# One step of a hybrid decoder: more expert blocks beside the gates, a layer's modulation computed elsewhere, slot transposes with a set place

## The chip, the cores and the metric

The kernel runs on one core of a Trainium2 chip. The metric is the device time of one execution in microseconds (us). The engines are TensorE (PE in the rows; PEld is its weight load), VectorE (DVE), ScalarE (ACT), GpSimd (POOL) and SyncE (SP). Each works through its own list of instructions in a fixed order, which a scheduler lays down when the kernel is built; an instruction that has to wait holds up those behind it on its engine.

## What is computed

Two layers of a decoder work on 576 tokens: a prompt of 512 and eight sampled sequences of 8. Cut to what matters here:

```
for l in range(2):
    mod = c @ w_ada + b_ada                      # modulation: shift, scale, gate, six parts
    hn  = rmsnorm(x) * (1 + scale1) + shift1
    proj = hn @ w_in                             # six parts: recurrence, short convolution, gates
    merged = sigmoid(ga) * rglru(conv(xa)) + sigmoid(gb) * (bg * conv(cg * xs))
    x  = x + g1 * (merged @ w_out)
    h  = rmsnorm(x) * (1 + scale2) + shift2
    # experts: per head the 16 best of 128 x 128 product keys
    idx, gate = top16(scores(h @ w_q, sub_keys))
    x  = x + g2 * sum_k gate_k * gelu(u_tab[idx_k] . h) * v_tab[idx_k]
y = rmsnorm(x)
```

There are 16384 experts a layer, in 128 blocks of 128. All products are exact to float32: an operand is split into a high and a low part and three products are added.

## The kernel before

**Tokens.** Of the 512 prompt tokens the first 384 (`TD`) go the dense way: all experts are computed for them and weighted with a gate matrix that is zero where an expert wasn't chosen. The last 128 and the 64 samples go by gathers: for each token and choice a row of `u_tab` and one of `v_tab` is fetched by GpSimd (`rows_of`, L659; 128 rows, 512 KB at a time) and used on VectorE (`udot` L665, `vsum` L676). These gathers are tasks in a list (`gtasks`). `pump` (L157) adds a number to a credit and hands out one task for each whole credit; calls of it stand all over the kernel, with rates from L65: `MPUMP` in the mixer, `QRATE` in the queries, `ARATE` in slots and gates, `BPUMP` per block in the second phase. What is left at the end of a layer is handed out in one go (L1039). A task's VectorE part is held behind the last split that was traced before it (`anchor`).

**A layer** runs through these stages, whose times are the profile's:

1. `mixer`. For 8 column groups six projections each (`proj`, L388). With each projection `beside` (L369) draws steps of a generator that runs the samples through the same layer (`chain`, `SIDE` steps a projection, 56 in all); when the chain is spent, it pumps gathers. In layer 0 it also computes one chunk of modulation: `ada` (L170) loads 1 MB of weights, multiplies, and evicts to a tile in the tag `rows`, which has five buffers that the gathered rows use too; `bring` (L196) turns the result to where it belongs. A layer has 24 chunks; 36 are done here, 16 of layer 0 and 20 of layer 1.
2. `queries` (L822): the second norm, the last four chunks of layer 1's modulation (layer 0 only), queries, scores and best 16.
3. `dense_slots` (L895): VectorE combines the halves (`combine`, L750), TensorE transposes the result into slots (L907), for three sets of 128 tokens.
4. `phase_a` (L911): the first `NA` expert blocks are multiplied with the tokens (`u_mm`, L707) and sent through a GELU. The first `NS_` of them go to DRAM (`ad`), the last 16 stay in SBUF, in two buffers of the tag `at`. Beside it the gate matrix is made in 24 pieces (`gate_piece`, L920): VectorE makes one-hot tiles (L930) and products (L935), TensorE multiplies them (L940), and the pieces go to DRAM. The odd ones of the first 18 use the `at` buffers as staging.
5. `phase_b` (L979): for each of the 128 blocks the activations are multiplied with the gates and then with the block's rows of `v_tab` (L1003). For the blocks from `NA` on the first product is made here too (`meet`, L987). They come first, then the 16 that were kept, then the spilled ones.

Loads of weights go through SP's queue, two tiles of 512 KB at a time, with six buffers for all of them (`load_pair`, L136). `split_blk` (L127) makes the two parts, the high one on ScalarE, the low one on VectorE. `tc.high_priority(offset=AHEAD)` lets the scheduler place instructions as if they stood 2000 earlier in the program.

Of the kernel before, what the change touches and what calls it, by code (L numbers as in the profile page):

```python
# [11 lines left out]
F32 = mybir.dt.float32  # L12
# [9 lines left out]
P = 128  # L22
L = 2
# [13 lines left out]
NA = 64  # L37
# [11 lines left out]
NB = 4  # L49
NOW = 0  # L50
TROW = 1
PACE = 0.8
# [11 lines left out]
SIDE = (2.5, 3.0)  # L64
MPUMP, QRATE, ARATE, BPUMP = 2.5, 0.0, 0.35, (2.9, 1.0)  # L65
# [6 lines left out]
def hybrid_step(ctx: ExitStack, tc: tile.TileContext, xT, cT, wada, vecs, fnorm, win, wout, wq, swin, swout, swq, subk,  # L72
# [133 lines left out]
    def settle():  # L206

        while late:
            late.pop()()
# [124 lines left out]
    def mixer_in(l, vt, mod, mx, hnh, hnl, mgf):  # L334
# [46 lines left out]

        todo = list(range(8, 48 - NB)) if l == 0 else []
# [311 lines left out]
    def peer(l, vt, mod):  # L694
# [4 lines left out]
        with tc.tile_pool(name=f"pg{l}", bufs=1) as pg:  # L699
# [6 lines left out]

            def u_mm(i, hi, lo):  # L707
                pu = (ubank if i < NA else small)(f"pu{l}_{i}")
                for k in range(KT):
                    w = slice(k * P, (k + 1) * P)  # L710
                    for (a, b) in ((hi, h2h), (hi, h2l), (lo, h2h)):
                        PE.matmul(pu[:, 0:TD], a[:, w], b[:, 0:NT, k, :],  # L712
                                  start=(k == 0 and a is hi and b is h2h), stop=(k == KT - 1 and a is lo))
                return pu

# [10 lines left out]
            with tc.tile_pool(name=f"pa{l}", bufs=1) as pa:  # L726
                svd = [pa.tile([P, 16, 16], F32, name=f"svd{t}") for t in range(NT)]
                sid = [pa.tile([P, 16, 16], U32, name=f"sid{t}") for t in range(NT)]
                with tc.tile_pool(name=f"pq{l}", bufs=1) as pq:
                    queries(l, vt, mod, pq, h2h, h2l, svd, sid, work_of)  # L730
                work_of.second(NG, finish)
                with tc.tile_pool(name=f"pk{l}", bufs=1) as pk:
                    dense_slots(l, pk, svd, sid, sl)
            with tc.tile_pool(name=f"pc{l}", bufs=1) as pc:
                with tc.tile_pool(name=f"pr{l}", bufs=1) as pr:
                    res = phase_a(l, pg, pc, pr, sl, gd, ad, u_mm)
                with tc.tile_pool(name=f"pb{l}", bufs=1) as pb:
                    phase_b(l, pg, pc, pb, g2, gd, ad, res, u_mm, h2h, h2l)
# [83 lines left out]
    def queries(l, vt, mod, pq, h2h, h2l, svd, sid, work_of):  # L822
# [15 lines left out]
        if l == 0:  # L838
            ada(1, range(24 - NB, 24))
            settle()  # L840

# [53 lines left out]
    def dense_slots(l, pk, svd, sid, sl):  # L895

        for t in range(NT):
# [13 lines left out]
    def phase_a(l, pg, pc, pa, sl, gd, ad, u_mm):  # L911
# [40 lines left out]
        for pr in range(NA // 2):  # L952
            raw = load_pair(uT[l, pr], f"u{l}_{pr}")
            i0 = 2 * pr // GI * GI
            if 2 * pr < NS_:
                ao = pg.tile([P, 2, TD], F32, tag="ao", bufs=2, name=f"ao{l}_{pr}")
            else:
                if i0 not in res:
                    res[i0] = pc.tile([P, GI, TD], F32, tag="at", bufs=2, name=f"at{l}_{i0}")
                ao = res[i0][:, 2 * pr - i0:2 * pr - i0 + 2, :]  # L960
            for u in range(2):
                i = 2 * pr + u
                hi, lo = split_blk(raw[u], f"u{l}_{i}")
                pu = u_mm(i, hi, lo)
                S.activation(ao[:, u, :], pu[:, 0:TD], AF.Gelu)  # L965
            if 2 * pr < NS_:
                S.dma_start(ad[pr], ao)
# [5 lines left out]
        while ti < len(tasks):  # L973
            with tc.high_priority(offset=NOW):
                tasks[ti][1]()
            ti += 1
        return res
# [193 lines left out]
```

## Time and profile before

| | us |
|---|---|
| median of 3 runs (lowest, highest) | 3758.79 (3755.74, 3765.05) |
| the profiled execution's own time | 3761.36 |
| its span, first to last instruction | 3759.6 |
| layer 0: mixer with output projection; queries | 40 to 580; 580 to 708 |
| layer 0: slots and first phase; second phase | 708 to 1133; 1133 to 1910 |
| layer 1: mixer with output projection; queries | 1948 to 2411; 2411 to 2524 |
| layer 1: slots and first phase; second phase | 2524 to 2954; 2954 to 3728 |

The profile is of one execution. "Busy" is the time that an engine's records cover; matmuls overlap in them, so what a matmul costs is read from start to start. The granted clock is the share of full speed that TensorE was given: 1.0 is 2.4 GHz, 0.5 is 1.2 GHz. Of an idle time the profile names the instruction whose end came last.

### The profile page before, as it was taken

The page shows a single profiled execution, that of the slowest core. Times are in us where ns is not written, and L with a number is a line of the kernel's source. Part 1 is how long each engine was busy: PE and PEld are TensorE (multiplying, and loading weights), DVE is VectorE, ACT ScalarE, POOL GpSimd, SP SyncE. Part 2 cuts the span into 40 slices and gives each one's busy share as a digit, 9 for nine tenths or more (in the row PEclk, how much of TensorE's full clock was granted, in tenths as well). Part 3 has the DMA queues.
Part 4 walks back from the last instruction along what each step waited for, and adds up shares of the span by engine and source line. Part 5 has one row for each costly group of instructions (what it writes and reads, how often), then busy time and mean ns, then how long its engine had stood idle before and what let it go on. Part 6 is the DMA issues. An engine that isn't in the chain of part 4 may idle for free.

```text
span 3759.6 us, 52675 instructions
## 1 busy us (share of the span) xinstructions
PE 3533.5 (94%) x18606; PEld 2936.9 (78%) x18606; DVE 2965.1 (79%) x6160; ACT 1494.4 (40%) x2032; POOL 1037.8 (28%) x830
## 2 busy tenths in 40 slices
PE   7998988998899999999979998899979999999998
PEld 5456677898599999988855586789957999998886
DVE  5235787999967888888873389899998788788887
ACT  3323344343763333333333244334456433333333
POOL 0000330232004444443320026213100355544331
PEclk9999899999599999999989999999957999999998
DMA  7876964686458999999956669549644899989994
GB/s 279 283 284 234 345 231 142 224 317 217 179 192 314 341 347 334 334 365 350 327 177 223 233 221 326 181 138 342 237 172 185 308 338 329 346 323 331 383 346 142
DMA packets 391145, 1026.41 MB, mean 273 GB/s; under 512 B 53984, under 2 KB 159584, under 8 KB 384096
## 3 DMA queue, kind: packets, MB, share of 16 engines
q1 hardware_dynamic: 266464, 551.13, 41.8%
q0 software_dynamic: 110592, 402.70, 29.7%
q10 hardware_dynamic: 13824, 69.21, 4.5%
q8 instruction: 146, 2.39, 0.2%
q14 instruction: 119, 0.97, 0.1%
HBM read 950.86 MB, written 72.01 MB: 272 GB/s over the span
## 4 chain that ended last, share of the span: by engine, by line
PE 48%; issue 15%; POOL 9%; DVE 9%; DMA 3%; ACT 1%; SPq 1%; POOLq 0%; ACTq 0%; DVEq 0%
PE pu L712 21%; PE pvo L1003 13%; PE pq L857 5%; POOL vrp L661 4%; POOL urp L661 4%; PE pj L150 3%; DVE A L935 3%; DVE oh L930 2%; POOL urs L661 2%; PE po L150 1%; DMA gt<-gd 1%; DMA raw_wi<-in_win_dram 1%; PE pgm L940 1%; PE pd L871 1%; DMA vrp<-in_vtab_dram,gidx 1%
## 5 line engine op out<-in xcount | busy, mean ns | idle before, releaser
L661 POOL DMA_INDIRECT urp<-in_utab_dram,gidx x256 | 366.3, 1431 | 600.5 <-DVE dot L667 467.5
L1003 PE MATMUL pvo<-hi_v,h2h 128*128 128x512 f32 x1536 | 487.7, 390 | 0.1
L661 POOL DMA_INDIRECT vrp<-in_vtab_dram,gidx x256 | 346.5, 1353 | 511.8 <-DVE accp L683 470.5
L1003 PE MATMUL pvo<-lo_v,h2h 128*128 128x512 f32 x1536 | 475.8, 389 | 0.0
L1003 PE MATMUL pvo<-hi_v,h2l 128*128 128x512 f32 x1536 | 465.6, 390 | 0.2 <-DVE h2l L1035 0.2
L661 POOL DMA_INDIRECT vrs<-in_vtab_dram,gidxs x128 | 156.1, 1219 | 762.6 <-DVE accs L683 301.0
L661 POOL DMA_INDIRECT urs<-in_utab_dram,gidxs x128 | 162.7, 1271 | 738.2 <-PE pm L186 316.3
L133 DVE TENSOR_TENSOR lo_v<-raw_v,hi_v 128x1024 fp32r<-128x1024 f32 x256 | 312.8, 1222 | 57.1 <-ACT hi_v L132 49.1
L712 PE MATMUL pu<-h2h,hi_u 128*128 128x384 f32 x1024 | 347.2, 339 | 1.6 <-ACT at L965 1.5
L712 PE MATMUL pu<-h2l,hi_u 128*128 128x384 f32 x1024 | 346.8, 339 | 0.0
L712 PE MATMUL pu<-h2h,lo_u 128*128 128x384 f32 x1024 | 346.6, 338 | 0.0
L712 PE MATMUL pu<-h2h,lo_ub 128*128 128x384 f32 x1024 | 343.1, 335 | 1.7 <-DVE lo_ub L133 1.6
L712 PE MATMUL pu<-h2h,hi_ub 128*128 128x384 f32 x1024 | 342.7, 335 | 0.0
L712 PE MATMUL pu<-h2l,hi_ub 128*128 128x384 f32 x1024 | 342.5, 334 | 0.0
L150 PE MATMUL pj<-hnh,hi_wi 128*128 128x512 f32 (+1 forms) x800 | 319.9, 401 | 18.7 <-ACT hi_wi L132 10.0
L1003 PEld LDWEIGHTS pvo<-lo_v,h2h 128*128 128x128 f32 x1536 | 288.4, 188 | 60.9
L1003 PEld LDWEIGHTS pvo<-hi_v,h2l 128*128 128x128 f32 x1536 | 288.1, 188 | 60.9 <-DVE h2l L1035 0.6
L1003 PEld LDWEIGHTS pvo<-hi_v,h2h 128*128 128x128 f32 x1536 | 287.3, 188 | 56.2 <-ACT h2h L1034 0.4
L683 DVE SCALAR_TENSOR_TENSOR accp<-vrp,dot,accp 128x1024 f32<-128x1024 f32 x252 | 322.7, 1281 | 6.1 <-DMA vrp<-in_vtab_dram,gidx 4.9
L150 PE MATMUL pj<-hnh,lo_wi 128*128 128x512 f32 (+1 forms) x800 | 314.4, 394 | 6.6 <-DVE lo_wi L133 6.4
L150 PE MATMUL pj<-hnl,hi_wi 128*128 128x512 f32 (+1 forms) x800 | 316.2, 396 | 3.1 <-DVE hnl L281 3.1
L667 DVE CUSTOM_DVE_ANT_0 urp<-urp,xt 128x1024 f32<-128x1024 f32 x256 | 304.7, 1218 | 5.7 <-DMA urp<-in_utab_dram,gidx 5.7
(439 smaller groups left out, 7210.3 us busy)
## 6 DMA issues: line engine op xcount, KB each, us to landing
raw_v<-in_vtab_dram SPq DMA_DIRECT2D x256, 512.0 KB
raw_u<-in_uT_dram SPq DMA_DIRECT2D x128, 512.0 KB
raw_ub<-in_uT_dram SPq DMA_DIRECT2D x128, 512.0 KB
raw_wi<-in_win_dram SPq DMA_DIRECT2D x96, 512.0 KB
gd<-stg ACTq DMA_DIRECT2D x48, 1024.0 KB
gt<-gd SPq DMA_DIRECT2D x768, 64.0 KB
raw_ada<-in_wada_dram SPq DMA_DIRECT2D x86, 512.0 KB
ad<-ao ACTq DMA_DIRECT2D x48, 384.0 KB
```

What stands on the lines that cost most here:

```text
L133: anchor[0] = V.tensor_tensor(out=lo, in0=raw, in1=hi.bitcast(F32), op=ALU.subtract).ins
L150: PE.matmul(out[:, c0:c1], a[:, w], b[:, k, c0:c1], start=(k == 0 and a is hi and b is xh), stop=(k == KT - 1 and a is lo))
L661: G.indirect_dma_start(out=rt, out_offset=None, in_=tab, in_offset=bass.IndirectOffsetOnAxis(ap=self.gidx[:, g, h, k:k + 1], axis=0))
L667: V.tensor_tensor_reduce(out=ur, in0=ur, in1=self.xt[g], scale=1.0, scalar=0.0, op0=ALU.mult, op1=ALU.add, accum_out=self.dot[:, g, h, k:k ...
L683: V.scalar_tensor_tensor(out=self.acc[g], in0=vr, scalar=w, in1=self.acc[g], op0=ALU.mult, op1=ALU.add)
L712: PE.matmul(pu[:, 0:TD], a[:, w], b[:, 0:NT, k, :], start=(k == 0 and a is hi and b is h2h), stop=(k == KT - 1 and a is lo))
L857: PE.matmul(pqs[:, t0 * P:t1 * P], a[:, w], b[:, t0:t1, k, :], start=(k == 0 and a is hi and b is h2h), stop=(k == KT - 1 and a is lo))
L871: PE.matmul(pd[:, t * P:(t + 1) * P], qt[:, t * P:(t + 1) * P], sk[:, u, :], start=True, stop=True)
L930: V.tensor_tensor(out=o, in0=iota2.unsqueeze(1).to_broadcast([P, 2, P, 2]), in1=slot(t, a, c0), op=ALU.is_equal)
L935: V.tensor_tensor(out=A[:, z], in0=oh[0], in1=slot(t, 2 + z, c0), op=ALU.mult)
L940: PE.matmul(pgm[:, n * P:(n + 1) * P], oh[1][:, n // 2, :, n % 2], A[:, z, n // 2, :, n % 2], start=(z == 0), stop=(z == 1))
L1003: PE.matmul(pv[t][q], a[:, tk], b[:, q * 512:(q + 1) * 512], start=(n == 0 and a is wh and b is vh), stop=(n == P - 1 and a is wl))
```

## The change

Expert blocks computed in the first phase go from 64 to 72, those spilled to DRAM from 48 to 56. The first 12 pairs of blocks are written down ahead of `dense_slots`, and the transposes of the three sets of slots are ordered behind the last matmul of blocks 14, 18 and 22 on TensorE. Layer 1's 24 chunks of modulation are computed in layer 0's `phase_a`, one with each pair of blocks from the 13th pair on; in layer 0's mixer the 16 chunks of layer 0 remain, and `queries` has none. `SIDE` goes from (2.5, 3.0) to (3.0, 3.5), `ARATE` from 0.35 to 0.3, `BPUMP` from (2.9, 1.0) to (3.0, 1.0).

```diff
-NA = 64
+NA = 72
 NS_ = NA - 16
...
-NB = 4
+TIES = (14, 18, 22)
...
-SIDE = (2.5, 3.0)
-MPUMP, QRATE, ARATE, BPUMP = 2.5, 0.0, 0.35, (2.9, 1.0)
+SIDE = (3.0, 3.5)
+MPUMP, QRATE, ARATE, BPUMP = 2.5, 0.0, 0.3, (3.0, 1.0)
...
             if todo:
-                n = todo.pop(0)
-                ada(n // 24, [n % 24])
+                ada(l, [todo.pop(0)])
...
-        todo = list(range(8, 48 - NB)) if l == 0 else []
+        todo = list(range(8, 24)) if l == 0 else []
...
+            def activations(pr, ao):
+                raw = load_pair(uT[l, pr], f"u{l}_{pr}")
+                for u in range(2):
+                    i = 2 * pr + u
+                    hi, lo = split_blk(raw[u], f"u{l}_{i}")
+                    pu = u_mm(i, hi, lo)
+                    S.activation(ao[:, u, :], pu[:, 0:TD], AF.Gelu)
+
+            def spilled(pr):
+                ao = pg.tile([P, 2, TD], F32, tag="ao", bufs=2, name=f"ao{l}_{pr}")
+                activations(pr, ao)
+                S.dma_start(ad[pr], ao)
...
-                    dense_slots(l, pk, svd, sid, sl)
+                    for pr in range(TIES[-1] // 2 + 1):
+                        spilled(pr)
+                    dense_slots(l, pk, svd, sid, sl, ends)
...
-        if l == 0:
-            ada(1, range(24 - NB, 24))
-            settle()
-
+        settle()
...
-            for n, s_ in enumerate((ii, jj, gg, gl)):
-                PE.transpose(pt[:, n * P:(n + 1) * P], s_, ident)
+            with tc.issue_after(ends[TIES[t]]):
+                for n, s_ in enumerate((ii, jj, gg, gl)):
+                    PE.transpose(pt[:, n * P:(n + 1) * P], s_, ident)
...
-        for pr in range(NA // 2):
-            raw = load_pair(uT[l, pr], f"u{l}_{pr}")
+        p0 = TIES[-1] // 2 + 1
+        for pr in range(p0, NA // 2):
             i0 = 2 * pr // GI * GI
             if 2 * pr < NS_:
-                ao = pg.tile([P, 2, TD], F32, tag="ao", bufs=2, name=f"ao{l}_{pr}")
+                spilled(pr)
             else:
                 if i0 not in res:
                     res[i0] = pc.tile([P, GI, TD], F32, tag="at", bufs=2, name=f"at{l}_{i0}")
-                ao = res[i0][:, 2 * pr - i0:2 * pr - i0 + 2, :]
...
+                activations(pr, res[i0][:, 2 * pr - i0:2 * pr - i0 + 2, :])
+            if l + 1 < L:
+
+                with tc.high_priority(offset=AHEAD):
+                    ada(l + 1, range(24 * (pr - p0) // (NA // 2 - p0), 24 * (pr - p0 + 1) // (NA // 2 - p0)))
```

`ends[i]` is the last matmul of block i, kept by `u_mm`.

## Rows read from the trace of the kernel before

**Rows 1.** The page, busy tenths in 40 slices of 94 us; PEclk is the granted clock.
```profile
PE   7998988998899999999979998899979999999998
...
PEclk9999899999599999999989999999957999999998
```

**Rows 2.** Windows, layer 0: length, busy (instructions) of PE, PEld, DVE, ACT, POOL; clock; DMA share; GB/s.
```profile
710.00:920.00 210.00, 209.33 (x1212) 208.06 (x1210) 205.22 (x629) 87.53 (x117) 64.97 (x50) 1.00 0.85 296
920.00:1040.00 120.00, 85.54 (x568) 55.21 (x569) 116.38 (x314) 76.42 (x76) 0.00 (x0) 0.51 0.37 154
1040.00:1133.00 93.00, 92.89 (x643) 88.21 (x644) 60.82 (x120) 54.57 (x67) 2.80 (x2) 0.97 0.56 201
1133.00:1657.00 524.00, 524.00 (x2649) 476.07 (x2650) 436.55 (x586) 188.80 (x257) 244.78 (x182) 1.00 0.94 337
1657.00:1910.00 253.00, 253.00 (x1125) 209.80 (x1124) 210.37 (x246) 90.93 (x120) 84.27 (x69) 1.00 0.94 337
```

**Rows 3.** Windows for the tile of expert blocks, `pu`: PE, PEld, ACT; clock; DMA.
```profile
708.00:920.00 212.00, 209.60 (x1200) 207.43 (x1198) 22.68 (x48) 1.00 0.85 295
920.00:1040.00 120.00, 0.26 (x1) 0.26 (x2) 0.80 (x2) 0.51 0.37 154
```

**Rows 4.** Waits, 920 to 1045 us: who waited for whom, us in total, times, longest.
```profile
PE pgm L940 <- DVE A L935: 17.0, 69, 1.5
...
PE ptd L908 <- DVE iid L797: 10.5, 1, 10.5
...
PE pu L712 <- ACT at L965: 1.5, 1, 1.5
```

**Rows 5.** Timeline of PE, 24 matmuls of a block apart: start, length, instruction.
```profile
912.63 0.33 PE L712 MATMUL pu<-h2h,lo_u 128*128 128x384 f32 x1
...
916.79 0.33 PE L712 MATMUL pu<-h2h,lo_u 128*128 128x384 f32 x1
```

**Rows 6.** Windows, both mixers: projections 1 to 23 and 24 to 48; columns as in rows 2.
```profile
40.10:318.90 278.80, 262.26 (x1443) 157.24 (x1444) 109.53 (x211) 95.61 (x151) 0.00 (x0) 0.97 0.76 266
318.90:518.10 199.20, 180.49 (x916) 134.90 (x914) 148.41 (x309) 74.92 (x105) 66.05 (x56) 0.91 0.81 291
...
1947.70:2193.30 245.60, 230.24 (x1039) 143.37 (x1040) 117.51 (x267) 89.72 (x132) 0.04 (x2) 0.97 0.62 214
2193.30:2345.50 152.20, 146.17 (x617) 116.28 (x615) 140.67 (x230) 65.70 (x87) 82.67 (x62) 0.99 0.82 292
```

**Rows 7.** Timeline of PE, layer 0's mixer: one chunk of modulation and one `bring`.
```profile
72.49 1.07 PE L186 MATMUL pm<-raw_ada,c 128*32 128x256 f32 x16
73.49 0.61 PE L200 MATMUL pt<-sel,ms 128*128 128x9 f32 x4
```

**Rows 8.** Windows, output projection to end of queries, both layers; columns as in rows 2.
```profile
519.80:708.00 188.20, 168.69 (x962) 137.29 (x963) 157.38 (x596) 67.35 (x120) 26.34 (x21) 0.95 0.45 157
...
2346.90:2524.20 177.30, 160.46 (x876) 132.08 (x877) 161.17 (x588) 66.46 (x115) 28.02 (x25) 0.95 0.45 155
```

**Rows 9.** Timelines at both layers' ends: last split, the next matmul; idle time in brackets.
```profile
1895.21 1.23 DVE L133 TENSOR_TENSOR lo_v<-raw_v,hi_v 128x1024 fp32r<-128x1024 f32 x1 [0.43 <-ACT hi_v L132]
...
1925.01 3.67 PE L719 MATMUL pf<-eye,accp 128*128 128x64 f32 x16 [14.61 <-DVE accp L683]
...
3727.84 1.89 PE L719 MATMUL pf<-eye,accp 128*128 128x64 f32 x16
```

**Rows 10.** Windows for L683 (sums of gathered rows), last split to last sum or product.
```profile
1896.40:1925.00 28.60, 20.52 (x16) 0.78 0.79 271
3714.00:3728.00 14.00, 6.36 (x5) 1.00 0.07 26
```

**Rows 11.** Waits, 330 to 450 us: ScalarE's eviction of a chunk.
```profile
ACT ms L192 <- DVE dots L667: 43.3, 7, 17.6
```

**Rows 12.** Timeline of PE: the first transposes of the first and second set of slots.
```profile
880.93 0.27 PE L908 MATMUL ptd<-ident,iid 128*128 128x128 f32 x1
...
918.35 0.27 PE L908 MATMUL ptd<-ident,iid 128*128 128x128 f32 x1
```

More of the change, by code (lines that the diff above doesn't have):

```diff
@@ L705, in peer @@
             work_of = Gathered(f"p{l}", gidx, gate, dot, {})
+            ends = {}
             def u_mm(i, hi, lo):
@@ L711, in u_mm @@
                     for (a, b) in ((hi, h2h), (hi, h2l), (lo, h2h)):
-                        PE.matmul(pu[:, 0:TD], a[:, w], b[:, 0:NT, k, :],
-                                  start=(k == 0 and a is hi and b is h2h), stop=(k == KT - 1 and a is lo))
-                return pu
+                        ends[i] = PE.matmul(pu[:, 0:TD], a[:, w], b[:, 0:NT, k, :],
+                                            start=(k == 0 and a is hi and b is h2h),
+                                            stop=(k == KT - 1 and a is lo)).ins
+                return pu
+            def activations(pr, ao):
[9 more added lines that the diff above has]
+                S.dma_start(ad[pr], ao)
             def finish(g, acc):
@@ L732, in peer @@
                 with tc.tile_pool(name=f"pk{l}", bufs=1) as pk:
-                    dense_slots(l, pk, svd, sid, sl)
+                    for pr in range(TIES[-1] // 2 + 1):
+                        spilled(pr)
+                    dense_slots(l, pk, svd, sid, sl, ends)
             with tc.tile_pool(name=f"pc{l}", bufs=1) as pc:
                 with tc.tile_pool(name=f"pr{l}", bufs=1) as pr:
-                    res = phase_a(l, pg, pc, pr, sl, gd, ad, u_mm)
+                    res = phase_a(l, pg, pc, pr, sl, gd, activations, spilled)
                 with tc.tile_pool(name=f"pb{l}", bufs=1) as pb:
@@ L893, in queries, with dense_slots @@
                               f"d{l}_{m}_{u}_{t}", tick)
-    def dense_slots(l, pk, svd, sid, sl):
+    def dense_slots(l, pk, svd, sid, sl, ends):
         for t in range(NT):
@@ L906, in dense_slots, with phase_a @@
             pt = small(f"ptd{l}_{t}")
-            for n, s_ in enumerate((ii, jj, gg, gl)):
-                PE.transpose(pt[:, n * P:(n + 1) * P], s_, ident)
+            with tc.issue_after(ends[TIES[t]]):
+                for n, s_ in enumerate((ii, jj, gg, gl)):
+                    PE.transpose(pt[:, n * P:(n + 1) * P], s_, ident)
             S.activation(sl[t].rearrange("p a b -> p (a b)"), pt, AF.Copy)
-    def phase_a(l, pg, pc, pa, sl, gd, ad, u_mm):
+    def phase_a(l, pg, pc, pa, sl, gd, activations, spilled):
         def tick(us):
@@ L959, in phase_a @@
                     res[i0] = pc.tile([P, GI, TD], F32, tag="at", bufs=2, name=f"at{l}_{i0}")
-                ao = res[i0][:, 2 * pr - i0:2 * pr - i0 + 2, :]
[L961 to L967, printed above, removed]
+                activations(pr, res[i0][:, 2 * pr - i0:2 * pr - i0 + 2, :])
+            if l + 1 < L:
+                with tc.high_priority(offset=AHEAD):
+                    ada(l + 1, range(24 * (pr - p0) // (NA // 2 - p0), 24 * (pr - p0 + 1) // (NA // 2 - p0)))
             while ti < len(tasks) and done <= total * (pr + 1) / (NA // 2 * PACE):
@@ L976, in phase_a @@
             ti += 1
+        settle()
         return res
```

## The prediction

> **What bounds the kernel now.** I read the slices of the page first [rows 1]: TensorE is busy nine tenths or more almost everywhere, except in two dips per layer; the dip that interests us here (slices 11 and 30) is also where the granted clock falls to about a half. So the first question for any edit is whether it takes work off TensorE in a stretch where TensorE is the limit, or only moves it within a stretch where something else is.
>
> The table by stretch answers that for layer 0 [rows 2]. From 710 to 920 us TensorE and VectorE are both full (VectorE 205 of 210). From 920 to 1040 us VectorE is full (116.4 of 120) and TensorE holds only 568 matmuls at a granted 0.51. From 1040 us to the end of the second phase at 1910 us TensorE is busy without a gap. Who does what in the dip: up to 920 us TensorE runs 1200 matmuls of the expert blocks, 24 to a block, so 50 blocks; in the dip it runs one [rows 3]. The waits say why [rows 4]: TensorE waits for VectorE's one-hot products (17.0 us, 69 times) and for the last slot transposes (10.5 us), and the next expert block starts only when ScalarE can write `at`. That last wait is a buffer: 48 of the 64 blocks go to DRAM, blocks 48 and 49 sit in the two PSUM buffers, and block 50 needs one of the two `at` buffers, which serve as staging for the odd gate pieces until piece 17 is out. So between block 50 and that moment TensorE has nothing to do but gates, at VectorE's pace.
>
> One block costs 24 steps of 0.173 us, 4.16 us at the 2.4 GHz level [rows 5]. A dip of about 120 us that holds some 43 us of gate matmuls at full clock (85.5 busy at half) is the room that the change can use.
>
> **The change, part by part.**
>
> *Layer 0's first mixer loses 20 of 36 modulation chunks and its sample chain is drawn faster (2.5 to 3 steps a projection).* Layer 1's mixer of the kernel before is the same work with no chunk and with 3 steps, so it is the template. It takes 245.6 + 152.2 = 397.8 us for its 48 projections, layer 0's takes 278.8 + 199.2 = 478.0 [rows 6]. Over the first 23 projections (23 chunks, no gathers yet) the difference is 33.2 us, 1.44 a chunk; over the rest (13 chunks, gathers running) 47.0 us, 3.6 a chunk. The sixteen that stay come first, before the gathers: 397.8 + 16 x 1.44 = 420.8, so **-57**. The other end is the chunk's own records, 1.07 + 0.61 = 1.68 us [rows 7]: 20 x 1.68 = -34.
>
> *The last 4 chunks leave the queries of layer 0.* From the output projection to the end of the queries layer 0 takes 188.2 us and layer 1 177.3 [rows 8]: **-11** (by the records -7).
>
> *Layer 1's mixer draws 3.5 steps instead of 3.* The chain of 56 steps then ends in 17 projections instead of 19; there is no row for it. TensorE is idle 15.4 of 245.6 us there [rows 6], so the gain is a few us at most; the loss is at most the cover of two projections, 2 x 5.4. I take **+2** (-5 to +10).
>
> *Eight more blocks per layer run beside the gates (72, 56 of them spilled).* What leaves the second phase, where TensorE has no gap, is 8 x 4.16 = 33.3 us a layer, **-66.6**. What it costs in the first phase: from the first block at 708 us to block 50 at 1040 us there are 332 us; 58 blocks (241) and 72 quarter pieces of gates at full clock (about 43) make 284, so 48 us remain and layer 1 can take all of it. VectorE, the engine that really sets the dip's end, gets 8 splits of 1.23 us more (9.8, [rows 9]), and loses gathers: the rate falls from 0.35 to 0.3, which by the counts below is 8 sums of 1.28 us fewer (10.3, [rows 10]). So **0** in layer 1 (-5 to +12). The extra spills are 3 MB a layer each way. They and the slightly faster gathers (3.0 for 2.9) meet transfers at a 0.94 share and 337 GB/s [rows 2], so a transfer limit is a rival, below.
>
> *The 24 chunks land in layer 0's first phase.* They want 24 x 1.44 to 3.6 = 35 to 86 us of TensorE where 48 are free. The dear price is due to a shared buffer: the evicted chunk sits in the `rows` tag with the gathered rows, and in the mixer ScalarE waited 43.3 us in 7 waits for VectorE's dot products before it could write one [rows 11]; on ScalarE the splits and evictions queue behind that wait, and TensorE waits for them. The chunks begin behind block 24, about 808 us, while gathers run until 920 us, so roughly half pay dear: about 60 us, 12 over the room, and 24 small additions on VectorE. I take **+14** (0 to +55). On SP's queue each chunk puts 1 MB between the expert loads, 25 MB in a stretch that is at a 0.85 share now [rows 3].
>
> The price of that room hangs on the clock. Before the dip 1.00 was granted, in it 0.51, after TensorE had run out of blocks [rows 3]. The Trainium skill (TensorE: Matmul & The Clock Gate, "What's actually happening") says that the slow state is the default and that activity releases it; the trace agrees. By that rule a filled dip stays at 2.4 GHz and the sum above stands; if the slow level is granted all the same, the late blocks cost double and the overflow is that of the first rival. The Trainium skill (DMA: Bandwidth & Descriptors, "Issuing engines are not separate DMA queues") speaks against the move: chunk loads on SP and gathers on GpSimd share the same 16 engines; no run here separates them yet.
>
> *The slot transposes may not go ahead of blocks 14, 18 and 22.* In the trace the first set starts at 881 us and the second at 918 us [rows 12], behind some 41 and 49 blocks, and the third after a wait of 10.5 us for VectorE [rows 4], in the dip. A bound lower than the place they have costs and gives nothing: **0**. (Behind a transpose that waits are queued the next expert blocks, and behind those, through the split buffers, VectorE's splits.) What it would be if the scheduler put them at the bound is the slow rival.
>
> *The gathers' budget.* Gathers are handed out by counters, so the number left for the end can be counted from the code. Before: 65 tasks in layer 0's mixer, 18 in the slots, 40 in the gates, 186 and 64 in the second phase, of 389: 16 left; layer 1: 6 left. The trace has 16 and 5 sums after the last split [rows 10]. After: 75 + 15 + 35 + 168 + 72, so 24 left; layer 1 (80 in the mixer) 19 left. Layer 0's sixteen take 28.6 us (1.79 each) and hold TensorE 14.6 us behind its last product; layer 1's hide, and its next matmul follows at once [rows 9]. Eight more cost 8 x 1.28 to 1.79 = 10 to 14 us. In layer 1 19 x 1.28 to 1.79 = 24 to 34 us, of which the 14 us from the last split to the end of the products are cover: 10 to 20. I take +13 and +17, **+30**.
>
> Sum: -57 - 11 + 2 - 66.6 + 0 + 14 + 30 = -88.6. The profiled execution's own time is 3761.4 us (span 3759.6), 2.6 above the median of the runs: 3761.4 - 88.6 - 2.6 = **3670**.
>
> **The rivals.**
> - *The first phase of layer 0 overflows*: every chunk at 3.6 and low clock in part, +55 instead of +14, so 3711. For it: the shared `rows` buffers [rows 11]; against it: after 920 us no gather runs.
> - *Slower: the transposes hold TensorE.* If the scheduler places them at blocks 14, 18 and 22, TensorE stops at about 772 us and waits for VectorE, whose slots came at 881, 918 and about 932 us [rows 4, 12]. From there remain 35 blocks, 43 us of gates and in layer 0 the chunks, 189 and 237 us, so block 58 comes at 1121 or 1169 instead of 1040: +81 and +129, the +14 inside, 3670 + 196 = 3866; if VectorE, freed of 27 splits, is earlier by 33 us and more, about 3750 to 3810. I take 3810. It turns the result slower once the two waits cost more than 89 us together.
> - *The second phase is limited by transfers.* By the code (512 KB a block for each table, 0.2 MB of gates, 0.2 MB of spill, 512 KB a gather) some 262 MB move in 744 us instead of 270 in 777: 1.4% more a second at a 0.94 share. If the rate can't rise, 11 us a layer are lost: 3692.
> - *The mixer gives back only the chunks' records* and the tails cost their full price: +23, +4, +4: 3701.
> - *Better*: no overflow and tails hidden behind the last transposes: 3670 - 14 - 20 = 3636.
>
> **How the numbers follow.** Forecast 0.55, overflow 0.15, transfers 0.08, records only 0.08, better 0.07, slower 0.07. The range from 3635 to 3715 holds most of all but the slow one, some 0.83. A measurement of this kernel tells about 0.3% from no change (11 us, the spread of the three runs): faster 0.90, same 0.03, slower 0.07.
>
> **What would show it.** Layer 0's mixer near 421 us and its queries near 177; 58 blocks before the first pause of the expert blocks; each second phase shorter by 33 us; about 24 and 19 sums behind the last split of each layer, with TensorE waiting some 28 and 17 us there. Wrong would be: TensorE waiting long for slots before block 58, ScalarE waiting for `rows` in the first phase, gaps between products in the second.

## The result, and the profile after

The changed kernel takes 3735.82 us (median; 3730.17 to 3744.92), the kernel before 3759.58 beside it: a ratio of 0.9938, interval 0.9920 to 0.9955. It is faster, clear of the interval, but by 24 us and not by 89. The profiled execution took 3730.17 us with a span of 3728.4, so the two profiles differ by 31.2 us. All that follows adds up to those 31.2; the median lies 5.7 us above the profiled execution, which was the fastest.

| us | before | after | difference | forecast |
|---|---|---|---|---|
| layer 0: mixer | 478.0 | 446.3 | -31.7 | -57 |
| output projection and queries | 189.9 | 176.4 | -13.5 | -11 |
| first phase with slots | 424.9 | 469.6 | **+44.7** | +14 |
| second phase | 777.5 | 744.1 | -33.4 | -33.3 |
| end, to layer 1's first projection | 37.3 | 51.6 | +14.3 | +13 |
| layer 1: mixer | 397.8 | 406.8 | +9.0 | +2 |
| output projection and queries | 178.7 | 178.3 | -0.4 | 0 |
| first phase with slots | 430.1 | 428.2 | -1.9 | 0 |
| second phase | 773.8 | 737.9 | -35.9 | -33.3 |
| end | 31.6 | 49.2 | +17.6 | +17 |

Seven rows came out within 3 us. The 57 us that are missing are the first phase of layer 0 (31), its mixer (25) and layer 1's mixer (7), less small gains elsewhere.

First the slices of the page after, which answer [rows 1]:

```profile
PE   7999989989999999999959999899999999999996
...
PEclk9999989989999999999979999999987999999998
```

The dip of layer 0 in slice 11 (clock 5 before) is gone. Layer 1's, in slices 30 and 31, is shallower (8 and 7 where 5 and 7 stood), and slice 21, the end of layer 0, shows 5 tenths of TensorE and clock 7. The windows of layer 0 after (length, busy and instructions of PE, PEld, DVE, ACT, POOL; clock; DMA share; GB/s) are projections 1 to 23, 24 to 48, output projection and queries, slots, the chunks' stretch, the rest of the first phase, and two parts of the second:

```profile
39.90:321.40 281.50, 262.06 (x1338) 156.02 (x1339) 119.14 (x281) 95.31 (x147) 0.00 (x0) 0.95 0.71 249
321.40:486.20 164.80, 150.67 (x621) 119.18 (x619) 143.73 (x236) 66.20 (x88) 82.96 (x63) 0.96 0.79 274
487.60:662.60 175.00, 164.32 (x887) 134.95 (x888) 158.85 (x654) 66.87 (x117) 18.56 (x16) 0.95 0.39 133
662.90:810.00 147.10, 133.08 (x789) 129.45 (x788) 143.11 (x532) 56.57 (x79) 39.73 (x15) 0.95 0.58 196
810.00:1020.00 210.00, 196.48 (x1524) 165.45 (x1528) 175.03 (x348) 111.43 (x139) 38.84 (x30) 0.93 0.92 336
1020.00:1132.00 112.00, 106.76 (x788) 93.81 (x789) 71.64 (x148) 61.61 (x79) 8.32 (x7) 0.96 0.78 273
1132.00:1564.00 432.00, 432.00 (x2202) 394.41 (x2201) 357.60 (x500) 154.51 (x210) 201.53 (x152) 1.00 0.95 341
1564.00:1876.00 312.00, 312.00 (x1386) 258.54 (x1384) 263.31 (x309) 114.19 (x150) 112.32 (x87) 1.00 0.94 342
```

Against [rows 2] two things stand out. The second phase is what it was: no gap on TensorE, the same transfers, only shorter. And from 810 to 1020 us a stretch has appeared that was not there: a DMA share of 0.92 at 336 GB/s with VectorE no longer full (175 of 210). What the engines and SP's queue waited for there, from 789 to 1028 us (who for whom, us in total, times, longest):

```profile
ACT stg L957 <- PE pgm L955: 52.2, 28, 6.6
ACT ms L192 <- PE pm L186: 30.9, 8, 14.4
...
PE ptd L923 <- DVE iid L814: 12.7, 1, 12.7
...
ACT ms L192 <- DVE accs L682: 1.9, 2, 1.7
...
SPq L141 <- PE pm L186: 124.0, 27, 25.6
```

ScalarE waited only 1.9 us for the buffer shared with the gathered rows, which the forecast had made the dear part. SP's queue waited 124 us in all, 25.6 at the longest, for TensorE to finish with load buffers that held chunks. What that longest wait did is read below, with the runs on loads and work.

The ends answer [rows 9, 10]: first the windows of L682 from the last split to the last sum, then the next matmul of each layer with its idle time.

```profile
1862.29:1905.20 42.91, 32.01 (x25) 0.69 0.88 310
3665.20:3694.00 28.80, 23.02 (x18) 0.78 0.72 248
```

```profile
1905.19 3.04 PE L734 MATMUL pf<-eye,accp 128*128 128x64 f32 x13 [28.94 <-DVE accp L682]
...
3694.01 3.67 PE L734 MATMUL pf<-eye,accp 128*128 128x64 f32 x16 [14.85 <-DVE accp L682]
```

There are 25 and 18 sums where 24 and 19 were counted ahead, and TensorE waits 28.9 and 14.9 us where 28 and 17 were named.

### The profile page after: what moved, and what is told of

It is laid out like the page before. It is cut to its first block, busy times and chain, and to the rows that moved or that the text cites. A ratio compares the mean times of both kernels' runs of the same rounds, so it can differ in the third digit from the quotient of the medians.

```text
span 3728.4 us, 52710 instructions
## 1 busy us (share of the span) xinstructions
PE 3501.1 (94%) x18606; PEld 2910.8 (78%) x18606; DVE 2961.9 (79%) x6160; ACT 1481.8 (40%) x2027; POOL 1119.1 (30%) x830
## 4 chain that ended last, share of the span: by engine, by line
PE 59%; issue 17%; POOL 11%; DVE 6%; DMA 5%; ACT 2%; POOLq 0%; SPq 0%; ACTq 0%; DVEq 0%
PE pu L713 22%; PE pvo L1016 14%; PE pj L150 8%; PE pq L871 5%; POOL vrp L660 4%; POOL urp L660 4%; POOL urs L660 3%; PE po L150 2%; PE pgm L955 1%; DMA raw_wi<-in_win_dram 1%; DVE A L950 1%; DVE oh L945 1%; PE pm L186 1%; DMA vrp<-in_vtab_dram,gidx 1%; DMA raw_ada<-in_wada_dram 1%
## 5 line engine op out<-in xcount | busy, mean ns | idle before, releaser
L660 POOL DMA_INDIRECT vrs<-in_vtab_dram,gidxs x128 | 217.8, 1702 | 789.1 <-DVE fid L786 373.4
L713 PE MATMUL pu<-h2h,hi_u 128*128 128x384 f32 x1152 | 397.7, 345 | 4.8 <-ACT hi_u L132 3.3
L713 PE MATMUL pu<-h2h,lo_u 128*128 128x384 f32 x1152 | 395.2, 343 | 2.3 <-DVE lo_u L133 2.3
L713 PE MATMUL pu<-h2l,hi_u 128*128 128x384 f32 x1152 | 395.7, 343 | 0.0
L660 POOL DMA_INDIRECT urs<-in_utab_dram,gidxs x128 | 171.8, 1342 | 670.2 <-issue 314.3
L682 DVE SCALAR_TENSOR_TENSOR accp<-vrp,dot,accp 128x1024 f32<-128x1024 f32 x252 | 322.7, 1280 | 12.0 <-DMA vrp<-in_vtab_dram,gidx 10.8
L713 PE MATMUL pu<-h2h,lo_ub 128*128 128x384 f32 x896 | 300.1, 335 | 0.0
L713 PE MATMUL pu<-h2h,hi_ub 128*128 128x384 f32 x896 | 299.9, 335 | 0.0
L713 PE MATMUL pu<-h2l,hi_ub 128*128 128x384 f32 x896 | 299.7, 334 | 0.0
```

The costliest lines, as they stand in the source:

```text
L660: G.indirect_dma_start(out=rt, out_offset=None, in_=tab, in_offset=bass.IndirectOffsetOnAxis(ap=self.gidx[:, g, h, k:k + 1], axis=0))
L682: V.scalar_tensor_tensor(out=self.acc[g], in0=vr, scalar=w, in1=self.acc[g], op0=ALU.mult, op1=ALU.add)
L713: ends[i] = PE.matmul(pu[:, 0:TD], a[:, w], b[:, 0:NT, k, :], start=(k == 0 and a is hi and b is h2h), stop=(k == KT - 1 and a is lo)).ins
```

## Experiments

The first phase of layer 0 is called A0 below, layer 1's A1. Stage times are from the profiles, and a single execution's span is compared with the 3728.4 us of after (the changed kernel). The five executions of after lie between 3730 and 3745 us, and the kernels whose first mixer is written as in after take 445 to 452 us for it: smaller differences of spans or mixers between single executions tell nothing. A0 repeats within 2 us where it is built alike (after and the two runs with more gathers).

### What the chunks cost where they went

**Chunks back.** Layer 1's chunks are computed in the mixer and queries again; all else as after.

```diff
-                ada(l, [todo.pop(0)])
+                n = todo.pop(0)
+                ada(n // 24, [n % 24])
...
-        todo = list(range(8, 24)) if l == 0 else []
+        todo = list(range(8, 44)) if l == 0 else []
...
+        if l == 0:
+            ada(1, range(20, 24))
...
-            if l + 1 < L:
+            if False:
```

> The changed kernel with layer 1's 24 chunks of modulation back where they were (20 in layer 0's mixer, 4 in its queries), all else as changed. Theory (in layer 0's first phase no chunk was hidden: the stretch went from 425 to 469 us, and layer 1's, without chunks, took 428): the first phase of layer 0 falls to about 428 us (-41), its mixer rises from 446 to 490 or more and its queries from 175 to 188, so the span is 10 to 25 us above the changed kernel's 3728, about 3745. Rival (the 44 us come from the new order of slots and blocks, and the chunks were hidden): the first phase stays near 469 us and the span is near 3785.

Measured: span 3747.5, as the theory had it. A0 is 423.7, so the 24 chunks cost 45.9 us there, 1.9 each. In exchange the mixer is 46.9 longer with them and the queries 12.3; these three stages net 13 us and the whole span 19. At the same place in the program the transfers are now at:

```profile
870.00:1080.00 210.00, 193.66 (x1314) 166.30 (x1313) 194.23 (x394) 122.13 (x136) 45.58 (x33) 0.83 0.71 274
```

**Work without loads, loads without work.** In the first the chunks multiply two tiles that already lie in SBUF; in the second every chunk is loaded, and of its work two matmuls of 8 columns each are left.

```diff
+            elif given:
+                raw = given
```

```diff
+            if only:
+                for u in range(2):
+                    PE.matmul(pm[0:32, 0:8], c32[:, 0, :], raw[u][:, 0:8], start=(u == 0), stop=(u == 1))
+                continue
```

> The changed kernel with the 24 chunks in layer 0's first phase multiplied, evicted and turned as before but without their loads: they read two tiles of tokens that lie in SBUF instead of 25 MB of weights, so layer 1's modulation, and what follows from it, is not the reference's. Theory (the chunks aren't hidden because their 1 MB loads take the six load buffers and the transfers, 0.92 share at 336 GB/s, from the blocks): layer 0's first phase falls from 469 to about 435 us. Rival (the stretch is full of work for TensorE and VectorE, and the chunks' 40 us of matmuls are simply added): it stays at 455 us or more.

> The counterpart: the 24 chunks are loaded, but only two small matmuls of 8 columns read each; the products, evictions and turns are left out and layer 1's modulation is set to zero, so its results are not the reference's. Theory (the loads and their buffers are the cost): layer 0's first phase stays at 455 to 470 us. Rival (the work is the cost): it falls to about 430.

Measured: A0 is 440.9 without loads (span 3708.3), nearer to the theory's 435 than to the rival's 455, and 459.2 without work (3723.2), in the theory's range. Over the 423.7 with no chunks that is 17 us for the work and 35 for the loads, 52 together where both cost 46: the loads cost about twice what the work costs. The windows of the same stretch, without loads and with loads alone:

```profile
812.00:984.00 172.00, 166.57 (x1448) 138.77 (x1447) 148.97 (x294) 91.31 (x121) 47.08 (x35) 0.99 0.80 284
```

```profile
810.00:1020.00 210.00, 187.05 (x1297) 165.18 (x1297) 171.79 (x344) 108.22 (x126) 35.87 (x29) 0.90 0.90 338
```

How the loads cost time can be read in the trace of after. SP's queue and TensorE between 739 and 805 us (start, length, instruction):

```profile
739.32 3.19 SPq L141 DMA_DIRECT2D raw_ada<-in_wada_dram  x2
756.36 5.29 SPq L141 DMA_DIRECT2D raw_ada<-in_wada_dram  x2
774.93 4.09 SPq L141 DMA_DIRECT2D raw_ada<-in_wada_dram  x2
804.63 1.18 SPq L141 DMA_DIRECT2D raw_u<-in_uT_dram  x2
...
803.11 0.45 PE L923 MATMUL ptd<-ident,iid 128*128 128x128 f32 x1 [12.74 <-DVE iid L814]
803.48 1.94 PE L186 MATMUL pm<-raw_ada,c 128*32 128x256 f32 x16
```

Three chunks, of two tiles each, hold all six load buffers. In TensorE's list the first of them stands behind the transposes of the third set of slots, and these wait for VectorE until 803.1 us. So SP loads the next two blocks only at 804.6 us, and no expert block is there to fill the wait. It isn't the transfers that are full in this stop (790 to 803 us, columns as above):

```profile
790.00:803.00 13.00, 0.37 (x4) 0.13 (x2) 12.93 (x22) 0.98 (x2) 10.61 (x4) 0.63 0.47 151
```

In the run with loads alone the same stop takes 20 of its 35 us:

```profile
PE ptd L929 <- DVE iid L820: 20.0, 1, 20.0
```

Without loads and with chunks back the third set stands behind 36 and 38 blocks and nothing waits for it. Counted on TensorE from start to start, the 46 us of A0 are 40.7 for the chunks' own matmuls and turns, 16.5 of added idle time (12.7 of them the stop) and 14.7 by which the expert blocks take longer, less 25.9 by which the gate products are shorter. The gates gain because the dip is gone: with chunks back the granted clock is 0.52 from 982 to 1052 us.

**The slots' transposes in another PSUM bank.** In after TensorE waits 12.7 us for the third set behind block 30, and blocks 31 onwards stand behind it.

```diff
-            pt = small(f"ptd{l}_{t}")
+            pt = bank(f"ptd{l}_{t}")
```

> The changed kernel with one edit: the transposed slots go to the four PSUM buffers of the tag bank, idle at that time, instead of the two of the tag small, which the chunks need. Theory (in layer 0 all transposes stand behind block 30 and TensorE stops 21 us there, because chunks that wait for a small buffer hold the six load buffers): the stop at block 30 goes, layer 0's first phase falls from 469 by 15 to 25 us, nothing else moves; ratio to the kernel before 0.987 to 0.990. Rival (the 41 us are just the chunks' work in a stretch that is full): the stop goes but the first phase stays within 8 us of 469.

Measured: 3724.92 us, ratio 0.9906 (0.9890 to 0.9923). The stop at block 30 is gone, the third set goes behind block 36, and A0 is 457.4, 12 less where 15 to 25 were expected. The interval of the whole kernel just meets that of after.

**Chunks spread over all pairs.** 8 or 12 of the 24 chunks go with the first 12 pairs, where the share is 0.58 (row 662.90 above).

```diff
                     for pr in range(TIES[-1] // 2 + 1):
                         spilled(pr)
+                        if l + 1 < L:
+                            with tc.high_priority(offset=AHEAD):
+                                ada(l + 1, range(8 * pr // 12, 8 * (pr + 1) // 12))
...
```

The call in `phase_a` hands out the chunks that are left.

> The kernel after with 8 of the 24 chunks of modulation moved ahead, one with two of every three of the first 12 pairs of blocks (663 to 810 us, where the DMA share is 0.58), and 16 left with the other 24 pairs. Theory 'the chunks cost what their loads can't find room for between 810 and 1020 us': 25 MB on top of the 274 GB/s of the run without chunks are 75 us at 336 GB/s and 13 MB of them fit; with 8.4 MB fewer there the overflow falls from 12 to 4 MB, so the first phase of layer 0 goes from 469.6 to 440 to 450 us and the kernel to about 3710. Rival 'a chunk's load holds two of the six load buffers until the chunk's turn on TensorE, wherever it stands': the price per chunk stays 1.9 us, the first phase stays within 8 us of 469.6.

> As spread8, with the slots' transposes in a PSUM bank of the ring. If the two savings add (the bank alone 12 us in the first phase), the first phase is 430 to 440 us and the ratio to the kernel before 0.983 to 0.986; if the bank only moves the stop that the chunks cause anyway, it is within 5 us of spread8.

> 12 chunks with the first 12 pairs, 12 with the other 24, and the bank. By the transfers no overflow is left in either stretch (12.6 MB in the first, where some 20 MB are free): 2 to 8 us less in the first phase than spread8_bank. If the chunks ahead delay the blocks that stand before the slots, and so VectorE's start on the gates, it is 5 us or more slower than that.

Measured: spread8 3717.67 us, ratio **0.9873** (0.9857 to 0.9890), A0 449.6; with the bank too 3721.34, 0.9887 (0.9871 to 0.9904), A0 449.8; with twelve and the bank 3714.57, **0.9865** (0.9849 to 0.9882), A0 446.0. All three ratios lie below that of after, with intervals that don't touch its own. The same two stretches in spread8, then the second in spread12_bank:

```profile
666.00:812.00 146.00, 146.00 (x922) 136.01 (x922) 143.05 (x540) 62.77 (x88) 30.78 (x17) 1.00 0.76 259
812.00:1020.00 208.00, 193.08 (x1496) 159.75 (x1495) 182.17 (x368) 113.04 (x137) 54.87 (x35) 0.93 0.92 341
```

```profile
812.00:1020.00 208.00, 194.02 (x1466) 167.15 (x1465) 183.44 (x366) 117.28 (x142) 52.46 (x33) 0.93 0.87 324
```

A0 loses 20 us, and the rival's number, "within 8 us of 469.6", falls. The transfer theory has the number, but its mechanism isn't seen: the share behind 812 us is 0.92 as before, as 35 gathers go where 30 went. What is visibly gone is the stop: TensorE works 146.0 of 146.0 us up to 812, where it worked 133.1 of 147.1, and no wait for slots is left. That the bank adds nothing to spread8 says the same: both take away one stop, which the crowd of chunks behind block 30 had made. So about 20 of the 46 us were the crowd and 26 are the chunks' remaining price. TensorE hardly waits for transfers in these 26: it is idle 15.7 us of A0 in spread8, and 16.3 with no chunk there. They are the chunks' own matmuls (40) and longer expert blocks (11), less what the gates gain (24).

### What the mixers gave

**The sample chain at its old speed.**

```diff
-SIDE = (3.0, 3.5)
+SIDE = (2.5, 3.0)
```

> The changed kernel with the sample chain drawn at the old rates, 2.5 and 3.0 steps a projection. Theory (drawing faster makes the mixers slower, not faster: with the chunks back layer 0's took 493 us at 3.0 against 478 at 2.5 in the kernel before, and layer 1's 407 to 413 at 3.5 against 398): layer 0's mixer falls from 446 to about 431 us, layer 1's from 407 to 398. By the counters 10 and 5 gathers more stay for the ends, 1.6 us each, +16 and +8, so the span is about the same, 3720 to 3735. Rival (the sixteen chunks that are left cost 3 us each whatever the chain does): the mixers stay within 6 us of 446 and 407, and the span rises to about 3750.

Measured: span 3742.5, between the two that were expected. The mixers fall to 429.5 and 394.8, by 17 and 12, as the theory had it; the queries of layer 0 rise by 10.6, the ends to 72.2 and 62.8, with 35 and 25 sums left instead of 25 and 18. The mixer's parts, projections 1 to 23 and 24 to 48 of layer 0:

```profile
39.40:311.70 272.30, 255.29 (x1322) 155.09 (x1323) 111.81 (x207) 95.85 (x148) 0.00 (x0) 0.96 0.74 256
311.70:468.90 157.20, 149.33 (x637) 117.82 (x635) 137.97 (x284) 68.72 (x89) 67.43 (x52) 0.98 0.72 250
```

With the chain at 2.5 steps, sixteen chunks cost 272.3 - 245.6 = 26.7 us over layer 1's row [rows 6], 1.67 each, near their own records [rows 7]; this is within what single executions differ by, so that 1.67 in place of 1.44 isn't shown. The faster chain costs 9 us in the first part and 8 in the second, and buys earlier gathers. It doesn't pay in the stage where it was booked; that it pays in the whole kernel isn't shown, since this one execution took 3744.24 us and the slowest of after 3744.92.

**A buffer of its own for the evicted chunk**, in the kernel before.

```diff
-            ms = st.tile([P, 256], F32, tag="rows", bufs=ROWS, name=f"ms{l}_{ch}")
+            ms = (own or st).tile([P, 256], F32, tag="ms" if own else "rows", bufs=2 if own else ROWS, ...)
```

> The kernel before with one edit: in the mixer a chunk is evicted to two buffers of its own instead of the five of the tag rows. Theory (the prediction's: a late chunk costs 3.6 us instead of 1.44 because ScalarE waits for a rows buffer that a gathered row holds): the 25 late projections of layer 0 fall from 199 to 165 to 175 us, the mixer from 478 to about 450. Rival (the late chunks are dear for another reason, such as VectorE's queue behind the scans and dot products): the mixer stays within 8 us of 478.

Measured: span 3754.1 beside 3759.6.

```profile
39.60:329.00 289.40, 269.13 (x1442) 160.43 (x1443) 109.04 (x211) 93.87 (x150) 0.00 (x0) 0.96 0.74 258
329.00:508.90 179.90, 173.16 (x916) 129.89 (x914) 143.55 (x302) 75.52 (x106) 63.83 (x50) 0.98 0.86 305
```

ScalarE's wait of 43.3 us [rows 11] is gone, and the second part loses 19 us where 24 to 34 were expected. But the first part takes 10.6 us longer, for no reason that the trace shows, and the whole mixer is only 8.7 shorter (469.3). So the wait is shown and its price in the mixer isn't; in A0, where I used that price, the wait was 1.9 us (above).

### What the eight blocks and the ends gave

**64 blocks in the new order.**

```diff
-NA = 72
+NA = 64
```

> The changed kernel with 64 blocks instead of 72 in the first phase, all else as changed. Theory: the two second phases give back what they gained, 33 us each (744 to 777 and 738 to 771), and layer 1's first phase stays at 428, since the blocks stood in a dip; in layer 0, whose first phase has no room left beside the chunks, it falls by up to 33 us (469 to 436). Span about 3728 + 67 - 33 = 3762. Rival (layer 0's first phase is bound by VectorE and by waits, not by TensorE's work): it stays near 465 and the span is near 3795.

Measured: span 3722.0, 6 us *less* than with 72; neither expected span came. The second phases are 33.6 and 33.8 us longer, as they had to be. Against that A0 is 21.1 shorter, A1 12.7, and the ends 26.2 and 18.6, with 8 and 2 sums left: with 72 blocks the second phase hands out sixteen gathers fewer (56 x 3 + 72 against 64 x 3 + 64), and the first phase has eight more blocks to load and split. So the eight blocks, taken alone, gave nothing that the measurement can tell.

**More gathers per block of the second phase**, and the same with the gate tile loaded only for the first group of a layer.

```diff
-MPUMP, QRATE, ARATE, BPUMP = 2.5, 0.0, 0.3, (3.0, 1.0)
+MPUMP, QRATE, ARATE, BPUMP = 2.5, 0.0, 0.3, (3.3, 1.15)
```

```diff
-            if pr == 0:
+            if pr == 0 and gt is None:
                 gt = pb.tile(...)
```

> The changed kernel with the second phase handing out more gathers, 3.3 a block and then 1.15 instead of 3.0 and 1.0. By the counters 56 x 3.3 + 72 x 1.15 = 268 for the 264 and 259 that are left, so none stays for the end. Theory (72 blocks instead of 64 took 16 gathers from the second phase's budget, and with 64 blocks the ends took 25 and 31 us instead of 52 and 49): the ends shrink by 26 and 18 us, the second phases stay at 744 and 738, span near 3684, ratio to the kernel before 0.979 to 0.983. Rival (the second phase has no transfers to spare: 0.94 share at 341 GB/s, and the added gathers ask for 15 to 20 GB/s more): the second phases grow by 15 us or more each and the span stays above 3705.

> The kernel after with more gathers handed out per block (as in the run tail) in which the tile of gate matrices that each group of the second phases loads is loaded only for the first group of a layer and used again; 25 MB a layer are not read, and the results are not the reference's. Theory 'the transfers hold the gathers back': with the DMA share of the second phase well below 0.95 the gathers keep up, the sums after the last value projection fall from 25 and 15 us to under 8, and the ends from 53.0 and 44.2 us to about 27; POOL's gathers in the first 430 us of layer 0's second phase rise above 154. Rival 'the rows buffers or the order written into VectorE set the pace': the share falls, the gathers stay within 5 of 154 and the sums after the last value projection within 4 us of 25 and 15.

Measured: by the counters none should be left in the first run, yet 25 and 15 sums are, and the time is 3729.86 us, ratio 0.9920 (0.9892 to 0.9947). The second phases take 744.1 and 737.9 us as in after, so that neither the theory nor the rival came true. In the second run 24 MB a layer are not read (720 loads of 64 KB), and the span is 3682.1: no sum is left, the ends are 15.0 and 25.6. The windows of 434 us from 1130 us on, more gathers, then fewer loads:

```profile
1130.00:1564.00 434.00, 434.00 (x2212) 396.23 (x2211) 358.88 (x503) 155.47 (x211) 202.74 (x154) 1.00 0.95 340
```

```profile
1130.00:1564.00 434.00, 432.72 (x2205) 394.81 (x2204) 382.56 (x530) 156.07 (x214) 241.87 (x171) 1.00 0.92 331
```

POOL issues 171 gathers where it issued 154 (153 in after). So a higher count doesn't raise the number of gathers in the second phase, and taking other loads away does. The traces tell why the count had no effect: VectorE's list in layer 0's second phase has the same number of dot products and sums ahead of each split of a value block in the first run as in after (counted from the start of the phase, 154 ahead of the 56th and 228 ahead of the 124th). The scheduler laid down the same order for both. And VectorE waited only 1.6 us for gathered rows there, so the transfers didn't hold it back. When the loads went, the scheduler drew another order, with 173 ahead of the 56th split and 258 ahead of the 124th; how much of the 41 us that this run gains over the first is the order and how much the freed transfers isn't separated.

### The order

**Pairs and transposes where they were before the change.**

```diff
-                    for pr in range(TIES[-1] // 2 + 1):
-                        spilled(pr)
...
-            with tc.issue_after(ends[TIES[t]]):
-                for n, s_ in enumerate((ii, jj, gg, gl)):
-                    PE.transpose(pt[:, n * P:(n + 1) * P], s_, ident)
+            for n, s_ in enumerate((ii, jj, gg, gl)):
+                PE.transpose(pt[:, n * P:(n + 1) * P], s_, ident)
```

> The changed kernel with the slots written down ahead of all blocks again and no tie of the transposes; 72 blocks and the moved chunks stay. Theory (tracing 12 pairs of blocks ahead moved the anchor that the gathers' sums are held behind, so VectorE came to the slots without them: in the changed kernel the last slots were there 143 us after the first block, before 226): the gathers' sums again stand between the slots' operations, the last slots come 200 us or more after the first block in both layers, layer 1's first phase stays near 430 us, and in layer 0, where the order has all transposes behind block 30, TensorE stands still from about 125 us after the first block until then: first phase 510 to 540 us, span 3770 to 3800. Rival (the prediction's sum, chunks hidden while VectorE works at the slots): layer 0's first phase near 440 us, span near 3700.

Measured: span 3736.1. A0 is 471.3, within 2 us of after, so that neither expected time came; A1 is 435.8, 7.6 more. In layer 1 the first set of slots goes to TensorE at 2665.98 us in this run and at 2598.11 in after, with the stage starting at the same moment within 0.2 us:

```profile
2665.98 0.27 PE L920 MATMUL ptd<-ident,iid 128*128 128x128 f32 x1
```

```profile
2598.11 0.27 PE L923 MATMUL ptd<-ident,iid 128*128 128x128 f32 x1
```

In after the three sets stand behind blocks 20, 28 and 30 (in layer 1 the third behind 39), later than the bounds 14, 18, 22. Here they stand behind 36, 44 and 50 in layer 1, so that the new order brought them forward; that it was the pairs and not the ties is only argued from the bounds, since this run takes both away. In layer 0 all three stand behind block 30 here, and TensorE waits 32.5 us for them: the stop at block 30 comes with the chunks and not with the new order.

### Two combinations

`best1` joins 64 blocks, the bank and the old chain; `na64_bank` the first two.

> The changed kernel with three edits: 64 blocks in the first phase, the slots in the PSUM tag bank, the sample chain at 2.5 and 3.0 steps. Theory (each does what it did alone: 64 blocks -6 us against the changed kernel, bank -6 to -12, the slower chain -17 and -12 in the mixers; by the counters 18 and 8 gathers stay for the ends, which costs 16 and up to 8 us against 64 blocks alone): span about 3698, ratio to the kernel before 0.982 to 0.986. Rival (the freed time is taken back at the ends, as with the slower chain alone): above 3715, 0.988 or more.

> The kernel after with 64 blocks beside the gates in place of 72 and the slots' transposes written into a PSUM bank of the ring in place of the small one. From 3724 us of the run with 64 blocks the bank takes the stop of the first phase of layer 0 away (12 us in the run that had it alone) and leaves the rest: 3708 to 3720, ratio 0.987 to 0.990. Rival 'what is freed in the first phase is given back at the next place where the order is drawn': 3722 to 3732, no better than either edit alone.

Measured: 3729.53 us, 0.9907 (0.9875 to 0.9939), and 3730.37 us, 0.9919 (0.9905 to 0.9932). In best1 the mixers keep their 427.7 and 394.2, but the ends are 44.2 and 33.6 and the queries of layer 0 188.1. In na64_bank TensorE's stop at block 30, 11.9 us in the run with 64 blocks, is gone, but TensorE waits 8 us for slots behind block 34, the pause of the expert blocks behind block 50 is 57 us where it was 38, and A0 is 450.9, 2 us longer. As both rivals had it, neither beats its parts.

## Why the prediction was right in direction and wrong in size

- **Second phases, -66.6**: -69.3. A block costs 24 steps of [rows 5], and nothing covered them. The rival that transfers would eat 11 us a layer did not come: the rows show 341 GB/s against 337 before.
- **Ends, +30**: +31.9, with the counted sums. The count also fits the runs with 64 blocks and with the old chain (8 and 2, 35 and 25 sums), but not the run with more gathers, where it leaves none and 25 and 15 stay; it gives the least that can be left, and that after lies on it is partly luck. What I did not see is that this and A1's +12.7 are the price of the eight blocks; I booked the fewer gathers of A1 as a gain of its own. Together with what 64 blocks give back in A0, the 67 us are gone (na64, one execution).
- **Layer 1's first phase, 0**: -1.9, right in size because two terms cancel, as I had it: +12.7 for eight blocks (I had 9.8 for the splits) and -14.6 for fewer gathers and the new order (I had 10.3 for the gathers).
- **Queries, -11**: -13.5.
- **Ties, 0**: the places lie behind the bounds, so the slower rival (TensorE stopped at block 14) did not come as stated. My reason was only half right: I took the old places, behind 41 and 49 blocks, to stay, and they moved to 20 and 28. And the rival's mechanism came in small, in layer 0: TensorE waited 12.7 us for slots behind block 30, the sign of being wrong that I had named, because chunks held the load buffers of the blocks behind.
- **Layer 0's mixer, -57**: -31.7. The step that failed is the template: "layer 1 at 3 steps" carries chunk-free projections over to a mixer with chunks. At 2.5 steps the mixer took 429.5, 9 above the 421 forecast; the faster chain made up the other 17 us. I had listed 2.5 to 3 as part of a gain and gave it no price of its own. The other end (-34, by the chunks' records) has the number by luck: with the chain at its old speed the same chunks gave back 48.5. The same edit in layer 1, priced at +2 (-5 to +10), cost 9 to 12.
- **Layer 0's first phase, +14**: +44.7, and this is the largest miss. The step that failed is the room: 48 us were counted on TensorE alone, and the 25 MB of loads were named and given no price. Two things were wrong in it. The loads hold the six load buffers: their price alone was 35 us, 20 of it the stop for slots, and spreading the chunks took 20 us off A0. And the chunks didn't fill the room: their own work was 41 us, less than the 48, but the gates gave back 26 us by the faster clock and TensorE's idle time grew by 17 instead of shrinking. The price of 3.6 us for a late chunk rested on the shared buffer, which cost 1.9 us there. So the overflow rival (+55) had about the right size by the wrong mechanism. My own later estimate, that 11 of the 25 MB don't fit beside 274 GB/s and cost 32 us (the transfer theory of spread8), comes near the 35 by luck: TensorE waited only 5.6 us for parts of expert blocks and 1.5 for chunks in A0 of after, the share was 0.47 in the stop, and loads alone ran at 372 GB/s from 809.7 to 830 us, above the 336 that I had taken for the limit.

On the clock the forecast held. TensorE was kept in work and 0.93 was granted from 810 to 1020 us, where the dip before had 0.51 [rows 3]; only behind the stop was it low (0.63 from 790 to 803 us). In layer 1, where TensorE runs out of blocks after the 58th, the granted clock is 0.57:

```profile
2766.30:2850.00 83.70, 68.00 (x456) 46.64 (x454) 79.45 (x215) 57.44 (x57) 2.15 (x2) 0.57 0.49 197
```

The Trainium skill (TensorE: Matmul & The Clock Gate, "What's actually happening") says that the slow state is the default and activity releases it, and both rows agree. By the Trainium skill (DMA: Bandwidth & Descriptors, "Issuing engines are not separate DMA queues") transfers that SP and GpSimd start run on the same 16 engines; no run here separates this from the load buffers.

## What to carry to other kernels

Work moved into another engine's idle time brings its loads along. Follow them through the buffers and the queue that they share with other loads, as carefully as the matmuls against free TensorE time: a load that comes early holds its buffers until its turn, and what is loaded behind it waits. Spread the moved work from the first place that has room. A change of pace (steps per projection, gathers per block) is an edit with a price of its own in each stage it touches, and a stage's gain counts only with what the next stages give back: here eight blocks gained 67 us in the second phases and lost as much in the first phases and the ends.

## What the runs showed of the hardware

SP's queue stood for 25.6 us behind six load buffers that held three chunks, and for 13 us of these (790 to 803) the transfers ran at a share of 0.47: full buffers, and not full transfers, kept TensorE from other work in its stop of 12.7 us. In the second phase a higher count of gathers in the program did not give more of them (154 in 434 us at 340 GB/s, 153 before), because the order on VectorE stayed the same. The wait of 12.7 us for one transpose was worth 12 us of the stage when another PSUM bank took it away, and the two remedies for it, bank and spread loads, did not add (449.6 and 449.8 us).
